# A fourth seven-product weight slab in every gate and up group, three more in the down projection, low parts subtracted by DMA

## The chip, the cores and the metric

The program runs on one core of a Trainium2 chip. The metric is device microseconds of that core for one execution. Five engines work side by side, each on its own instruction queue in a fixed order: TensorE (PE; its weight loads are shown as PEld), VectorE (DVE), ScalarE (ACT), GpSimd (POOL, which here only issues DMAs) and SyncE (SP, which issues the weight loads). A DMA moves data between memory and the on-chip buffers; an accumulating DMA adds what it reads to what lies at its destination, and only POOL issues those here.

## The reference, cut to what matters

One layer of an encoder on 256 rows of width 2048. The change touches its last third, the SwiGLU feed-forward block of inner width 5632, and the final norm behind it:

```python
def swiglu(h, w_gate_up, w_down):
    gate, up = jnp.split(h @ w_gate_up, 2, axis=-1)
    return (jax.nn.silu(gate) * up) @ w_down
...
        x = x + swiglu(rms_norm(x, norm_g[l, 2]), w_gate_up[l], w_down[l])
    return rms_norm(x, final_norm_g)
```

All arithmetic is float32. The mixers and the cross attention ahead of it are not touched.

## The kernel before

**Products.** A float32 operand is held as two parts: the high part is its rounding to the matmul's format, made by a ScalarE cast, the low part is what that rounding left, made by a VectorE subtraction. One product of two operands is three matmuls into the same PSUM bank: high by high, high by the weight's low part `wl`, low by high (`part`, L433 to L435). In the feed-forward block the activations are the stationary side (128 rows by 128) and the weights move, 512 columns at a time.

**Slabs and halves.** The weights come in 252 slabs of 16 blocks of 128x128 (1 MB), in the order of use. `Stream` loads a slab into one of three `raw` tiles and makes `wh` (ScalarE cast) and `wl` (VectorE subtraction) from it in pieces called halves. `_fill` (L167 to L171) writes out the instructions for the half that is used next and for three more; `_buffers` has three pairs of buffers in `wp` and one in the extra pool, so four halves exist at a time, and the cast of a half waits until TensorE has used up the half four before it.

**Plain slabs (N).** Two halves of 1024 columns. A slab is four activation tiles k by one group of 512 columns c; with two blocks of 128 rows each, it is 8 products, 24 matmuls.

**Paired slabs (S).** A slab is two tiles k by both column groups, again 8 block products, done in seven by a Strassen-like scheme: 21 matmuls. The sums of weight blocks that this needs are made in `_sums` (L140 to L163), the sums of activation blocks once for each pair of tiles in `combine` (tiles `z`, in the profile also `y`). A paired slab has four halves of 1024, 512, 1024 and 1024 columns, for 2, 1, 2 and 2 products. Ahead of the third half stand the additions of weight blocks on VectorE, in place in `raw`, so they wait for the casts and subtractions of the first two halves. Where the slab's number is in `SUMMED` (all paired gate and up slabs) DMAs have made part of the sums in a tile `two`: two loads on SP and one accumulating DMA on POOL (L101, L102), issued one slab ahead; two additions are left. Otherwise (the down slabs) there are four.

**Order.** `paired_rows` goes through a string of N and S. The feed-forward block has 11 groups of gate and up columns; the first goes by plain slabs, the other ten by `GROUP`, eight slabs each. In a group `mixed` (L1064 to L1071) takes the four PSUM banks of the seven-product sums out on VectorE after the last S, `gated` and `upped` (L1073 to L1084) add the other four, apply SiLU and multiply, and `up` (L1057 to L1062) turns the result on VectorE and stores it to the DRAM tensor `hidden`: twelve VectorE instructions in all. Two sets of four banks swap their roles from group to group. The down projection is two passes of 22 slabs, `PASSES`, of which the last three slabs (LATE) are left for `down_end`.

**Reloaded tiles.** `fetch` (L1087 to L1103) brings `hidden` back in the turned layout, 44 tiles `f[k]`: a load on POOL (`load_turned`), a cast on ScalarE and a subtraction on VectorE (`split`), the first 22 during the gate and up groups, the rest as the first down pass asks for them (`ready`). f[22] to f[27] lie in the tiles `z`, f[28] to f[43] in those of the block's input, `h3`, so they can be written only when the gate and up groups are done with them. In the down passes `combine` first adds the two parts of f[k] and f[k+1] on VectorE again.

**The scheduler.** A compiler pass lays each engine's instructions out in a fixed order, by the order in which the program states them and by when it expects them to be ready. `mark` and `keep_place` bind a stretch of instructions to the stated order.

**The end.** `down_end` adds the last blocks of one quarter of the columns through an identity matmul (`split`), runs 12 tiles f[k] (four from the stream, eight from the tiles `held`) by two blocks of rows, 72 matmuls, and norms each block of rows (`norm`).

## Time and profile before

| | |
|---|---|
| median of 3 runs | 1438.75 us (1436.18 to 1439.48) |
| the profiled execution | 1435.07 us, of which its span is 1433.3 us |
| TensorE, VectorE, ScalarE, POOL busy | 1423.0, 1146.2, 815.2, 234.8 us |
| mean granted TensorE clock | 0.999 |
| gate and up groups 2 to 11 | about 780 to 1193 us of the span |
| first and second down pass | about 1193 to 1309 and 1309 to 1407 us |

In the rows of the profile an engine's group of instructions has its line, its engine, its operation, `out<-in`, and in a timeline the start and length in us, the count, and in brackets how long the engine stood idle before it and what ended that. Neighbouring instructions overlap a little at their ends, so the distance from one start to the next is what one costs the engine.

### The profile page before, as it was taken

To read this page: it belongs to the slowest core of one execution; us is meant where nothing else is said; L and a number is where in the kernel's file an instruction comes from. 1 tells how busy PE (TensorE), PEld (TensorE's weight loads), DVE (VectorE), ACT (ScalarE), POOL (GpSimd) and SP (SyncE) were. 2 spreads that over 40 slices of the span, in tenths; PEclk is the share of its full clock that TensorE was granted. 3 is DMA by queue.
4 is the path that set the end of the run, shared out by engine and by line. 5 is a ranking of instruction groups with operands and counts; after the bars stand their busy time and mean duration, and the time that the engine had idled before them with its cause. 6 is when DMAs were issued, how large, how long until landed. Compare 5 with 4: busy or idle time off the path is not lost.

```text
span 1433.3 us, 18652 instructions
## 1 busy us (share of the span) xinstructions
PE 1423.0 (99%) x6589; PEld 1180.7 (82%) x6589; DVE 1146.2 (80%) x1738; ACT 815.2 (57%) x1183; POOL 234.8 (16%) x306
## 2 busy tenths in 40 slices
PE   9999999999999999999999999999999999999997
PEld 8888888888888888888888888888888888888886
DVE  6667868777877767777677888898888888989997
ACT  7556565446645555556554656555555556655655
POOL 0000100013212223531431121122011002000000
PEclk9999999999999999999999999999999999999999
DMA  9876564546667788964986999889999887655554
GB/s 352 299 285 248 205 206 162 175 169 224 202 196 236 234 267 252 274 200 166 289 239 209 286 286 277 278 275 282 294 293 288 268 260 229 219 230 179 193 218 147
DMA packets 73037, 343.79 MB, mean 240 GB/s; under 512 B 10957, under 2 KB 12654, under 8 KB 45168
## 3 DMA queue, kind: packets, MB, share of 16 engines
q1 hardware_dynamic: 54848, 288.98, 57.5%
q0 software_dynamic: 17664, 52.97, 15.8%
q8 instruction: 51, 0.84, 0.2%
q10 hardware_dynamic: 432, 0.66, 0.1%
q14 instruction: 42, 0.34, 0.1%
HBM read 322.12 MB, written 20.45 MB: 239 GB/s over the span
## 4 chain that ended last, share of the span: by engine, by line
PE 97%; DVE 1%; ACT 0%; DMA 0%; issue 0%; SPq 0%; ACTq 0%
PE pg L433 22%; PE pg L434 22%; PE pg L435 22%; PE pm L434 7%; PE pm L435 7%; PE pm L433 7%; PE pg L381 4%; PE pg L382 2%; PE pm L1344 1%; PE pm L1022 1%; PE pm L993 1%; DMA raw<-in_W 0%; PE pm L1753 0%; DVE res L283 0%; PE pm L994 0%
## 5 line engine op out<-in xcount | busy, mean ns | idle before, releaser
L136 DVE TENSOR_TENSOR wl<-raw,wh 128x1024 fp32r<-128x1024 f32 (+1 forms) x413 | 494.8, 1212 | 166.1 <-ACT wh L135 163.2
L135 ACT CAST wh<-raw 128x1024 fp32r<-128x1024 f32 (+1 forms) x413 | 424.5, 1043 | 283.9 <-PE pg L435 196.4
L433 PE MATMUL pg<-wh,act 128*128 128x512 f32 (+1 forms) x1191 | 465.6, 391 | 0.0
L434 PE MATMUL pg<-wl,act 128*128 128x512 f32 (+1 forms) x1191 | 463.9, 389 | 0.4 <-DVE wl L136 0.2
L435 PE MATMUL pg<-wh,act 128*128 128x512 f32 (+1 forms) x1191 | 463.9, 389 | 0.0
L433 PEld LDWEIGHTS pg<-wh,act 128*128 128x128 f32 x1191 | 223.8, 188 | 47.8 <-issue 1.5
L434 PEld LDWEIGHTS pg<-wl,act 128*128 128x128 f32 x1191 | 223.8, 188 | 47.2 <-DVE wl L136 1.3
L435 PEld LDWEIGHTS pg<-wh,act 128*128 128x128 f32 x1191 | 223.7, 188 | 47.2 <-DVE act L283 0.4
L159 ACT CAST wh<-raw 128x1024 fp32r<-128x1024 f32 (+1 forms) x150 | 137.0, 921 | 146.8 <-DVE raw L157 46.4
L160 DVE TENSOR_TENSOR wl<-raw,wh 128x1024 fp32r<-128x1024 f32 (+1 forms) x150 | 156.1, 1061 | 57.0 <-ACT wh L159 56.8
L434 PE MATMUL pm<-wl,act 128*128 128x512 f32 x309 | 120.5, 390 | 0.1
L433 PE MATMUL pm<-wh,act 128*128 128x512 f32 x309 | 120.2, 389 | 0.0
L435 PE MATMUL pm<-wh,act 128*128 128x512 f32 x309 | 120.2, 389 | 0.0
L381 PE MATMUL pg<-act,wh 128*128 128x512 f32 x256 | 90.5, 395 | 0.0
L382 PE MATMUL pg<-act,wl 128*128 128x256 f32 x256 | 71.8, 280 | 0.0
L434 PEld LDWEIGHTS pm<-wl,act 128*128 128x128 f32 x309 | 58.0, 188 | 13.0 <-DVE wl L136 0.6
L433 PEld LDWEIGHTS pm<-wh,act 128*128 128x128 f32 x309 | 58.0, 188 | 12.0
L435 PEld LDWEIGHTS pm<-wh,act 128*128 128x128 f32 x309 | 58.0, 188 | 12.0
L102 POOL DMA_DIRECT2D two<-in_W x30 | 26.6, 887 | 241.2 <-DMA two<-in_W 116.0
L157 DVE TENSOR_TENSOR raw<-raw 128x512 f32<-128x512 f32 x90 | 62.0, 689 | 1.3
L159 ACT CAST wh<-two 128x1024 fp32r<-128x1024 f32 x30 | 31.6, 1052 | 51.1 <-PE pg L435 21.7
L381 PEld LDWEIGHTS pg<-act,wh 128*128 128x128 f32 x256 | 48.1, 188 | 10.5
(375 smaller groups left out, 1821.9 us busy)
## 6 DMA issues: line engine op xcount, KB each, us to landing
raw<-in_W SPq DMA_DIRECT2D x216, 1024.0 KB, 5.6
raw<-in_W SPq DMA_DIRECT2D x30, 768.0 KB, 6.1
two<-in_W SPq DMA_DIRECT2D x60, 256.0 KB, 4.9
two<-in_W POOLq DMA_DIRECT2D x30, 512.0 KB, 9.3
raw<-in_W SPq DMA_DIRECT2D x11, 512.0 KB, 7.6
hidden<-g POOLq DMA_DIRECT2D x22, 256.0 KB, 3.7
tmp<-hidden POOLq DMA_DIRECT2D x44, 128.0 KB, 5.4
features<-tmp POOLq DMA_DIRECT2D x32, 128.0 KB, 5.3
```

Of the source, the lines that this page charges most:

```text
L102: nc.gpsimd.dma_start(t, W[:, 512:1536], accum_op=ALU.add)
L135: nc.scalar.copy(wh[:, a:b], r[:, a:b])
L136: nc.vector.tensor_tensor(out=wl[:, a:b], in0=r[:, a:b], in1=wh[:, a:b].bitcast(F32), op=ALU.subtract)
L157: nc.vector.tensor_tensor(out=out, in0=a, in1=b, op=ALU.add)
L159: nc.scalar.copy(wh, src)
L160: nc.vector.tensor_tensor(out=wl, in0=src, in1=wh.bitcast(F32), op=ALU.subtract)
L381: self.nc.tensor.matmul(p[:, :], wh, slot[:, :], start=start, stop=False)
L382: self.nc.tensor.matmul(p[:, 0:R], wl, slot[:, 0:R], start=False, stop=stop)
L433: self.nc.tensor.matmul(p, hi, wh, start=start, stop=False)
L434: self.nc.tensor.matmul(p, hi, wl, start=False, stop=False)
L435: self.nc.tensor.matmul(p, lo, wh, start=False, stop=stop)
L993: nc.tensor.matmul(p[:, :], q[d][:, r * P:(r + 1) * P], kt[d][:, :], start=d == 0, stop=False)
```

## The change

- **Groups.** `GROUP` goes from `NNSNSNSN` to `NSNSsNSN`: four of eight slabs in seven products. The small s is a paired slab outside `SUMMED`: loaded whole, its four additions made on VectorE. A fourth combination tile `z3` is added, made from h3[6] and h3[7]; tiles 8 to 15 instead of 6 to 15 are left to the plain slabs.
- **Down passes.** Eight and ten paired slabs instead of six and nine. The plain slabs of the first pass begin at f[16] instead of f[12].
- **Low parts by DMA.** `split_far` casts the high part on ScalarE, writes the negated operand to the low part on ScalarE, and adds the operand by an accumulating DMA on POOL. It replaces the VectorE subtraction for all 44 reloaded tiles (in no kept place) and in the combinations of the down passes. Those also take their operands from `hidden` by two loads on POOL instead of two additions on VectorE.
- **Order.** Each product of `paired_rows` is kept in its stated place. In `down_end` each block of rows is, and the identity matmuls move from ahead of the first block of rows to ahead of the second.

```diff
-GROUP = "NNSNSNSN"
+GROUP = "NSNSsNSN"
-PASSES = "NNNNSNNSNNSNNSNNSNNSNN", "NSNSNSNSNSNSNSNSNSNNNN"
+PASSES = "NNNNSNSNSNNSNSNSNNSNSN", "NSNSNSNSSNSNSNSNSSNNNN"
...
-          for i, x in enumerate(plan) if x == "S"}
-SUMMED = {i for i in PAIRED if i < DOWN}
+          for i, x in enumerate(plan) if x in "Ss"}
+SUMMED = {GATE_UP + 8 * j + i for j in range(10) for i, x in enumerate(GROUP) if x == "S"}
...
+    def split_far(self, hi, lo, src):
+
+        self.nc.scalar.copy(hi, src)
+        self.nc.scalar.mul(lo, src, -1.0)
+        self.nc.gpsimd.dma_start(lo, src, accum_op=ALU.add)
+
...
-    def combine(self, z, a, b):
+    def combine(self, z, a, b, src=None):
 
         tt, t, u, v, w = self.tt, *(self.tmp() for _ in range(4))
-        for x, y in ((t, a), (u, b)):
-            tt(x, y[:, 0:R].bitcast(F32), y[:, R:512].bitcast(F32), ALU.add)
-        yield SOON
+        if src:
+            for x, k in zip((t, u), src):
+                self.load_turned(x, self.ff, k)
+            yield 8.0
+        else:
+            for x, y in ((t, a), (u, b)):
+                tt(x, y[:, 0:R].bitcast(F32), y[:, R:512].bitcast(F32), ALU.add)
+            yield SOON
...
-        self.split2(hi[:, 0:R], lo[:, 0:R], v)
+        split = self.split_far if src else self.split2
+        split(hi[:, 0:R], lo[:, 0:R], v)
...
+            mark = self.mark()
             self.part(q[name][:, :], hi, lo, wh, wl, new, left[name] == 0)
+            self.keep_place(mark)
...
-                    mark = self.mark()
-                    self.split(f[k - ahead], m.pop(k - ahead))
-                    self.keep_place(mark)
+                    t = f[k - ahead]
+                    self.split_far(t[:, 0:R], t[:, R:512], m.pop(k - ahead))
...
-        sums = [((2 * i, 2 * i + 1), z[i]) for i in range(GROUP.count("S"))]
+        z = z + [gp.tile([P, 1024], F32R, name="z3")]
+        sums = [((2 * i, 2 * i + 1), z[i]) for i in range(4)]
...
-                yield from self.combine(x, *(f[k] for k in ks))
+                yield from self.combine(x, *(f[k] for k in ks), ks)
...
-        mark = self.mark()
-        for j, parts in split:
-            for a in parts:
-                nc.tensor.matmul(ps[1][:, j:j + R], self.identr, a, start=False, stop=False)
-        self.keep_place(mark)
...
         for r in range(2):
+            mark = self.mark()
+            for j, parts in split if r else ():
+                for a in parts:
+                    nc.tensor.matmul(ps[1][:, j:j + R], self.identr, a, start=False, stop=False)
             for k, wh, wl in held:
                 self.part_rows(ps[r], r, f[k], wh, wl, False, k == FT - 1)
+            self.keep_place(mark)
             norm(ps[r], r)
```

More of the change, by code (lines that the diff above doesn't have):

```diff
@@ L449, in combine @@
         hi, lo, x4 = self.forms(z, a)
-        self.split2(hi[:, 0:R], lo[:, 0:R], v)
+        split = self.split_far if src else self.split2
+        split(hi[:, 0:R], lo[:, 0:R], v)
         if hi.shape[1] == 512:
-            self.split2(hi[:, R:512], lo[:, R:512], w)
+            split(hi[:, R:512], lo[:, R:512], w)
         else:
-            self.split2(hi[:, R:], lo[:, R:], w[:, 0:P])
-            self.split2(*x4, w[:, P:R])
+            split(hi[:, R:], lo[:, R:], w[:, 0:P])
+            split(*x4, w[:, P:R])
     def forms(self, z, a):
@@ L490, in paired_rows @@
                 before(i)
-            if kind == "S":
+            if kind in "Ss":
                 ks, z = next(todo)
```

## The prediction

> **What bounds the kernel now.** I read the page first, then the stretches of the feed-forward block, then timelines of one paired slab and of one group's end.
>
> ```profile
> span 1433.3 us, 18652 instructions
> PE 97%; DVE 1%; ACT 0%; DMA 0%; issue 0%; SPq 0%; ACTq 0%
> 780.00:1193.00 413.00, 412.94 (x1821) 341.31 (x1820) 354.52 (x417) 233.28 (x270) 67.55 (x79) 1.00 0.90 277
> 1157.20:1198.70 41.50, 41.50 (x185) 34.37 (x184) 35.30 (x42) 23.19 (x25) 2.51 (x4) 1.00 0.70 228
> 1193.00:1309.00 116.00, 115.97 (x509) 94.80 (x508) 107.05 (x176) 68.33 (x102) 12.98 (x15) 1.00 0.63 212
> 1309.00:1407.00 98.00, 98.00 (x434) 81.12 (x434) 94.09 (x133) 56.69 (x69) 0.00 (x0) 1.00 0.57 210
> ```
>
> The chain that ended last is 97% TensorE. The rows of stretches give length, then busy us (count) of PE, PEld, DVE, ACT, POOL, the granted clock, DMA share and GB/s. TensorE has no gap in the gate and up groups (first row), and the clock is full. VectorE is busy 86% there, 92% in the first down pass, 96% in the second. So matmuls taken out shorten the time, one for one, as long as VectorE keeps ahead.
>
> ```profile
> 1396.78 0.39 PE L433 MATMUL pg<-wh,f 128*128 128x512 f32 x1
> 1401.54 0.39 PE L433 MATMUL pm<-wh,act 128*128 128x512 f32 x1
> 1151.60 0.39 PE L433 MATMUL pm<-wh,act 128*128 128x512 f32 x1
> 1193.08 0.39 PE L433 MATMUL pg<-wh,f 128*128 128x512 f32 x1
> ```
>
> The first two rows are the first matmuls of the last paired slab of the second down pass and of the plain slab behind it: 4.76 us for 21 matmuls, 0.2267 us each. The other two bound the last gate and up group: 41.48 us for 183, the same 0.2267. A product (three matmuls) is 0.68 us, a plain slab 5.44.
>
> **The gain.** Ten gate and up slabs and three down slabs lose a product each: 13 x 0.68 = 8.84 us (6.80 and 2.04). The identity matmuls only move.
>
> **VectorE on average.** One cycle of the second down pass, plain then paired, in its steady state:
>
> ```profile
> 1386.82 1.05 ACT L159 CAST wh<-raw 128x1024 fp32r<-128x1024 f32 x1 [1.17 <-PE pm L435]
> 1388.18 2.00 ACT L135 CAST wh<-raw 128x1024 fp32r<-128x1024 f32 x2 [0.31 <-PE pm L435]
> 1397.02 1.05 ACT L159 CAST wh<-raw 128x1024 fp32r<-128x1024 f32 x1 [1.17 <-PE pm L435]
> 1387.90 1.23 DVE L160 TENSOR_TENSOR wl<-raw,wh 128x1024 fp32r<-128x1024 f32 x1 [0.82 <-ACT wh L159]
> 1389.26 2.36 DVE L136 TENSOR_TENSOR wl<-raw,wh 128x1024 fp32r<-128x1024 f32 x2
> 1391.54 1.82 DVE L160 TENSOR_TENSOR wl<-raw,wh 128x1024 fp32r<-128x1024 f32 x2
> 1393.28 2.87 DVE L157 TENSOR_TENSOR raw<-raw 128x512 f32<-128x512 f32 x4
> 1396.06 1.22 DVE L160 TENSOR_TENSOR wl<-raw,wh 128x1024 fp32r<-128x1024 f32 x1
> 1398.10 1.23 DVE L160 TENSOR_TENSOR wl<-raw,wh 128x1024 fp32r<-128x1024 f32 x1 [0.82 <-ACT wh L159]
> ```
>
> From start to start, a 1024-column subtraction costs VectorE 1.14 us (1389.26 to 1391.54 is two), the 512-column one 0.60, the four additions 2.78. A paired slab with four additions is 3 x 1.14 + 0.60 + 2.78 = 6.80 us of VectorE for 4.76 us of TensorE; a plain slab 2.28 for 5.44. So s for N adds 4.52 us of VectorE to a group: the last group goes from 35.30 to 39.8 of 40.8 us, 98%, where no reloaded tile falls. Earlier groups also lose the subtraction for their reloaded tiles, 22 of them to this stage:
>
> ```profile
> L291 ACT CAST f<-tmp x14: 400/401/403, 880.2 to 1010.2; 128x256 fp32r<-128x256 f32 x14
> L283 DVE TENSOR_TENSOR f<-tmp,f x14: 414/419/422, 881.4 to 1011.6; 128x256 fp32r<-128x256 f32 x14
> L283 DVE TENSOR_TENSOR tmp<-f 128x256 f32<-128x256 f32 x6 | 2.5, 419 | 0.0
> L283 DVE TENSOR_TENSOR y<-tmp,y 128x256 fp32r<-128x256 f32 (+1 forms) x6 | 2.1, 351 | 0.0
> L283 DVE TENSOR_TENSOR f<-tmp,f 128x128 fp32r<-128x128 f32 x3 | 0.9, 288 | 0.0
> ```
>
> At 0.42 us each that is 9 us over six groups (and as much in the first down pass). In the down passes a combination loses two additions and its low parts, 2.5 + 2.1 + 0.9 = 5.5 us for three, 1.8 each, by the last three rows here. Nine old ones give 16.5 us back against three more slabs at 4.52; so the down passes end with less VectorE work, and there the trade holds on average. In the gate and up groups it holds on average too, by 1 us a group. The average isn't what decides, I think; the four buffers are.
>
> **Two paired slabs in a row (`Ss` in each group, `SS` twice in the second pass).** Call T the start of a paired slab on TensorE. The slab at 1396.78 gets its fourth low part at 1398.10, T+1.32: its cast waited for a buffer that TensorE frees as it enters the slab (1397.02, "PE"). The slab before started ten us earlier (45 matmuls, at 1386.58), and behind it the next half's subtraction began at 1389.26, T+2.68, because its cast at 1388.18 again waited for TensorE. So however idle VectorE was, it starts on the next slab at T+2.68. Where that is a paired slab with four additions: first half done at 3.82, second at 4.42, additions at 7.20, third half at 8.42. TensorE wants that third low part after 21 + 9 matmuls and one more: T+4.76+2.04+0.23 = 7.03. It is 1.39 late. If the scheduler puts two additions behind the third half, the fourth half pays: all of it on VectorE ends at T+9.56, wanted at 8.39, 1.17 late. Nothing covers this: the order of the products is kept, so TensorE can't take a later one first. I take 1.3 us (1.17 to 1.39): ten groups 13.0 us (11.7 to 13.9), two places in the second pass 2.6 (2.3 to 2.8).
>
> **The group's head.** Before, two plain slabs stood behind a group's end; now a paired one is second.
>
> ```profile
> 1151.70 1.22 DVE L136 TENSOR_TENSOR wl<-raw,wh 128x1024 fp32r<-128x1024 f32 x1
> 1152.83 0.68 DVE L283 TENSOR_TENSOR g<-g,pg 128x512 f32<-128x512 f32 x1
> 1153.43 1.28 DVE L283 TENSOR_TENSOR h<-h,pg 128x512 f32<-128x512 f32 x2
> 1154.63 1.41 DVE L287 SCALAR_TENSOR_TENSOR h<-h,rc,g 128x512 f32<-128x512 f32 x2
> 1155.95 1.30 DVE L557 STREAM_TRANSPOSE g<-h 128x512 f32<-128x512 f32 x2
> 1157.17 1.19 DVE L136 TENSOR_TENSOR wl<-raw,wh 128x1024 fp32r<-128x1024 f32 x1
> ```
>
> TensorE begins the group at 1151.60 = E (third row of the matmuls above). VectorE works without a gap through the last group's evacuation and turning until 1157.17, E+5.57. The half at 1151.70 is the third of the new group, now the paired slab's first. Behind the burst come its second half (0.60), two additions (0.70 each), third and fourth half (1.14 each): third done at E+8.7, fourth at E+9.8. TensorE wants the third at 5.44+2.04+0.23 = E+7.7 and the fourth at 9.07: some 1.0 late. Bounds: 0 if the last four instructions of the burst (1154.63 to 1157.17, 2.5 us) are put behind, 1.9 if the additions stand so that the fourth cast starts after the third subtraction. I take 1.0 for the nine groups that follow such an end: 9.0 (0 to 17).
>
> **POOL, and the start of the down projection.** Each far-made part adds one POOL issue, each combination five:
>
> ```profile
> L564 POOL DMA_DIRECT2D tmp<-hidden x44 | 38.8, 889 | 53.7 <-issue 24.4 <-DMA hidden<-g 13.3 <-DVE act L283 10.0
> two<-in_W POOLq DMA_DIRECT2D x30, 512.0 KB, 9.3
> tmp<-hidden POOLq DMA_DIRECT2D x44, 128.0 KB, 5.4
> POOL two L102 <- DMA two<-in_W: 113.1, 14, 11.7
> 1206.68 0.39 PE L433 MATMUL pg<-wh,z 128*128 128x512 f32 x1
> 1203.71 0.75 DVE L283 TENSOR_TENSOR z<-tmp,z 128x256 fp32r<-128x256 f32 x2
> PEld pg L433 <- ACT act L299: 0.6, 2, 0.3
> ```
>
> 94 more issues (44 + 10 x 5) at 0.889 are 84 us of a queue that stood idle most of the stage, no loss by themselves. ScalarE gets 44 negations, at 0.40 us if they cost what the cast of that size does, and those of the combinations, in idle time too (it is busy 233 of the 413 us). An accumulating DMA of 128 KB isn't in the trace; between the load of that size and the 512 KB accumulation it lands 5.4 to 9.3 us after its issue, where the subtraction took 0.4. That matters in one place: f[22] was subtracted at 1203.71 and wanted at 1206.68, a cover of 3 us, and with eight tiles more in pairs it is wanted 5.4 us sooner. Against that, the tile `z` it lies in comes free a slab earlier, and the work is no longer bound to its place. Small waits exist already (0.6 us in the last row). I take 1.0 us, bounds 0 and 6 (one full landing).
>
> By the Trainium skill (DMA: Bandwidth & Descriptors, "Anatomy of one DMA — SWDGE (gpsimd) path") a DMA from this queue takes 2.0 us and its bytes at 436 GB/s, an estimate of 2.3 us for 128 KB; this trace's 5.4 us for such a load is over twice that, and by the page the 1.0 would be 0 and the sum 1 us lower.
>
> **The end.** The last VectorE chain was just in time:
>
> ```profile
> PEld pm L1244 <- DVE tmp L283: 0.3, 1, 0.3
> 1410.79 1.89 DVE L127 TENSOR_TENSOR held<-raw,held 128x512 fp32r<-128x512 f32 x3
> ```
>
> The identity matmuls waited 0.3 us; moving them saves at most that. But with two paired slabs ahead VectorE reaches its end chain about as late as the second `SS` made it, and what waits next is the `held` low parts, which queue on VectorE behind that chain. I take +1.0 (−0.3 to 3).
>
> **The sum.** −8.84 + 13.0 + 2.6 + 9.0 + 1.0 + 1.0 = +17.8 us. On the profiled execution's 1435.07: 1452.8. The median of the runs, 1438.75, lies 3.7 above that execution, so the forecast is 1456.5. All lower bounds give +4.9 (1443.6), all upper ones +33.9 (1472.6).
>
> **Rivals.**
>
> 1. *Faster: VectorE keeps ahead.* If the scheduler spreads the additions and the burst so that neither place stalls, all of the gain stays: 1438.75 − 8.84 = 1429.9. For it: VectorE stays below TensorE's time on average, and the second pass already ran at 96% without a loss. Against it: there each paired slab has a plain one before it, and T+2.68 is set by buffers, which no order of VectorE changes. It decides as soon as both stalls together are under 0.4 us a group. Chance 0.14. The Trainium skill (Perfetto Trace Analysis, "Identifying the Most-Contended Engine") judges VectorE by its occupancy, and by that rule alone this rival would be the forecast; the same page says under "Optimization Strategy" that a gap that repeats can mean too few buffers, and the rows of the casts agree with that.
> 2. *About the same.* `Ss` costs its lower bound, the rest nothing but for half the group heads: within 3 us of 1438.75 only if the stalls come to 6 to 12 us in all, half of what I count. Chance 0.07.
> 3. *Slower still: POOL's order.* A far-made part waits on POOL for a load (5.4 us) and ScalarE. Where it stands ahead of a `two` accumulation, this comes up to 6 us late, and the paired slab with it. Once in each of the six groups that reload tiles, 4 us each: +24 on the forecast, 1480. For it: POOL is one queue in order, and `two` lands only 9.3 us after issue. Against it: POOL already waits up to 11.7 us for the loads of `two`, and far-made parts can fall into that. Chance 0.13.
>
> The forecast itself has 0.66. A measurement of this kernel can't tell 0.2% (2.9 us) from no change. Faster 0.15, same 0.06, slower 0.79. The forecast's own range is 1443 to 1473; to leave no more than 2 in 10 out I widen it toward the first two rivals and a little toward the third: 1433 to 1477.
>
> **What would show it.** Right: in the gate and up groups, waits of TensorE's weight loads for `wl` (L160) that sum to some 15 to 30 us, in the third and fourth half of the s slab and of each group's first paired slab; a group of 42 to 44 us; TensorE's count down by 39 matmuls; two such waits in the second pass; POOL without long waits on the path. Wrong: groups of 40.8 us with no wait (rival 1); waits for `two` or for f tiles in place of `wl` (rival 3); a first down pass longer than 118 us, or an end chain more than 3 us late.

## The result and the profile after

| | before | changed |
|---|---|---|
| median of the runs (5 each) | 1436.33 us | 1538.40 us |
| lowest and highest run | 1436.10, 1439.48 | 1535.57, 1539.58 |
| span of the profiled execution | 1433.3 us | 1537.4 us |
| mean granted TensorE clock | 0.999 | 0.983 |

The changed kernel takes 1.0702 times as long (1.0683 to 1.0720): 102 us more, where 18 were forecast. The page of the changed kernel (last row: DMA issues, KB each, median us to landing):

```profile
span 1537.4 us, 18834 instructions
...
PE 1455.7 (95%) x6550; PEld 1180.1 (77%) x6550; DVE 1180.6 (77%) x1739; ACT 857.9 (56%) x1288; POOL 318.2 (21%) x400
...
PE 70%; DVE 11%; DMA 8%; issue 5%; POOL 3%; ACT 2%; SPq 0%; ACTq 0%; POOLq 0%; DVEq 0%
...
tmp<-hidden POOLq DMA_DIRECT2D x64, 128.0 KB, 6.8
```

The waits of TensorE's weight loads in it, us in total, times and longest:

```profile
PEld pg L440 <- DVE wl L160: 34.3, 29, 6.6
PEld pm L440 <- DVE wl L160: 30.2, 29, 2.4
PEld pg L439 <- ACT wh L159: 20.4, 14, 3.4
PEld pm L439 <- ACT wh L159: 20.3, 14, 3.7
```

The matmuls went from 6589 to 6550, the 39 of the plan. The chain that ended last is TensorE's for 70% in place of 97%. TensorE waits for low parts of paired slabs, as forecast, for 64 us, but also 41 us for their high parts, which ScalarE makes, and no term of the forecast stood for that. VectorE's share of the span fell from 80% to 77%, though the waits name it. The Trainium skill (Perfetto Trace Analysis, "Identifying the Most-Contended Engine") looks for the engine with the highest occupancy, and judges TensorE's headroom by, among others, the busy share of its weight loads. Both figures are 77% here, so the rule doesn't tell TensorE and VectorE apart, and it passes over ScalarE at 56%, whose work TensorE waits for too.

Stretches of the changed kernel (length, busy us and counts of PE, PEld, DVE, ACT, POOL, granted clock, DMA share, GB/s): the eighth and the fifth of the ten groups that have paired slabs, the last, the first and the second down pass.

```profile
1125.71:1171.97 46.26, 42.64 (x181) 33.48 (x180) 39.52 (x48) 24.49 (x27) 7.74 (x9) 1.00 0.85 259
976.47:1027.77 51.30, 45.63 (x181) 35.33 (x180) 39.51 (x48) 26.96 (x35) 11.17 (x13) 0.93 0.85 237
1217.70:1275.07 57.37, 45.13 (x182) 34.40 (x180) 39.59 (x50) 35.72 (x65) 27.48 (x31) 0.91 0.86 227
1275.07:1405.81 130.74, 121.03 (x506) 96.24 (x504) 100.80 (x137) 73.06 (x119) 45.31 (x51) 0.96 0.77 226
1405.81:1510.97 105.16, 98.87 (x427) 79.57 (x426) 97.73 (x126) 59.62 (x77) 5.81 (x7) 1.00 0.56 196
```

A group has 180 matmuls, 40.81 us without a wait. A group took 46 us where nothing else falls into it, 51 where reloaded tiles do, 57 at the end. VectorE has the same 39.5 us of work in all three, so its load doesn't tell them apart; ScalarE's and POOL's columns do.

Counting the matmuls of the timeline off against the plan gives each stall its place (a stall is what a stretch has over its matmuls times 0.2267 us; in the last column but one, 17.8 us stand ahead of the first matmul of the first pass, in "groups alone" 11.7):

| stalls of TensorE, us | before | changed | groups alone | far-made reloads alone | changed, own reloads | down passes alone |
|---|---|---|---|---|---|---|
| group 1 | 0 | 5.5 | 1.0 | 2.4 | 4.1 | 0 |
| groups 2 to 6 | 0.5 | 50.5 | 17.6 | 28.3 | 25.4 | 2.1 |
| groups 7 to 9 | 0.1 | 15.3 | 8.7 | 0 | 14.8 | 0.5 |
| group 10 | 0 | 16.6 | 2.9 | 16.4 | 4.9 | 0 |
| first down pass | 1.0 | 16.5 | 17.5 | 7.2 | 53.0 | 31.1 |
| second down pass | 0 | 8.6 | 0 | 0 | 10.2 | 8.6 |
| end | 0.3 | 1.0 | 1.5 | 0.3 | 1.1 | 1.0 |
| sum | 1.9 | 113.9 | 49.2 | 54.6 | 113.5 | 43.3 |

112 us more of stalls, 8.8 less of work and 1.5 of a later start of the groups come to the 104 us between the two spans, within 1. The columns further right are experiments that follow.

### The profile page after: what moved, and what is told of

It is laid out like the page before. It is cut to its first block, busy times and chain, and to the rows that moved or that the text cites. A ratio compares the mean times of both kernels' runs of the same rounds, so it can differ in the third digit from the quotient of the medians.

```text
span 1537.4 us, 18834 instructions
## 1 busy us (share of the span) xinstructions
PE 1455.7 (95%) x6550; PEld 1180.1 (77%) x6550; DVE 1180.6 (77%) x1739; ACT 857.9 (56%) x1288; POOL 318.2 (21%) x400
## 4 chain that ended last, share of the span: by engine, by line
PE 70%; DVE 11%; DMA 8%; issue 5%; POOL 3%; ACT 2%; SPq 0%; ACTq 0%; POOLq 0%; DVEq 0%
PE pg L440 17%; PE pg L441 16%; PE pg L439 16%; DMA tmp<-hidden 5%; PE pg L387 4%; DVE wl L160 4%; PE pm L440 4%; PE pm L441 3%; PE pm L439 3%; DVE wl L136 3%; PE pg L388 2%; DVE raw L157 2%; DMA hidden<-g 1%; POOL tmp L578 1%; DMA raw<-in_W 1%
## 5 line engine op out<-in xcount | busy, mean ns | idle before, releaser
L136 DVE TENSOR_TENSOR wl<-raw,wh 128x1024 fp32r<-128x1024 f32 (+1 forms) x387 | 465.2, 1213 | 168.5 <-ACT wh L135 166.5
L135 ACT CAST wh<-raw 128x1024 fp32r<-128x1024 f32 (+1 forms) x387 | 399.7, 1042 | 273.5 <-PE pg L441 197.9
L439 PE MATMUL pg<-wh,act 128*128 128x512 f32 (+1 forms) x1166 | 457.5, 393 | 5.1 <-ACT wh L159 3.9
L441 PE MATMUL pg<-wh,act 128*128 128x512 f32 (+1 forms) x1166 | 455.3, 390 | 0.0
L159 ACT CAST wh<-raw 128x1024 fp32r<-128x1024 f32 (+1 forms) x202 | 184.7, 923 | 155.6 <-DVE raw L157 58.0
L160 DVE TENSOR_TENSOR wl<-raw,wh 128x1024 fp32r<-128x1024 f32 (+1 forms) x202 | 211.6, 1066 | 71.5 <-ACT wh L159 71.0
L439 PEld LDWEIGHTS pg<-wh,act 128*128 128x128 f32 x1166 | 219.7, 188 | 54.9 <-ACT wh L159 6.5
L441 PEld LDWEIGHTS pg<-wh,act 128*128 128x128 f32 x1166 | 219.5, 188 | 45.7 <-DVE act L283 0.2
L440 PE MATMUL pm<-wl,act 128*128 128x512 f32 x284 | 113.3, 399 | 8.5 <-DVE wl L160 8.5
L439 PE MATMUL pm<-wh,act 128*128 128x512 f32 x284 | 112.9, 397 | 5.7 <-ACT wh L159 5.6
L441 PE MATMUL pm<-wh,act 128*128 128x512 f32 x284 | 111.4, 392 | 0.0
L157 DVE TENSOR_TENSOR raw<-raw 128x512 f32<-128x512 f32 x142 | 98.0, 690 | 3.1
L578 POOL DMA_DIRECT2D tmp<-hidden x64 | 61.5, 1053 | 101.1 <-ACT tmp L1172 50.7
L439 PEld LDWEIGHTS pm<-wh,act 128*128 128x128 f32 x284 | 54.3, 191 | 20.1 <-ACT wh L159 8.7
L441 PEld LDWEIGHTS pm<-wh,act 128*128 128x128 f32 x284 | 54.0, 190 | 10.8
L160 DVE TENSOR_TENSOR wl<-two,wh 128x1024 fp32r<-128x1024 f32 x30 | 36.7, 1225 | 30.1 <-ACT wh L159 30.1
```

Of the source, the lines that this page charges most:

```text
L135: nc.scalar.copy(wh[:, a:b], r[:, a:b])
L136: nc.vector.tensor_tensor(out=wl[:, a:b], in0=r[:, a:b], in1=wh[:, a:b].bitcast(F32), op=ALU.subtract)
L157: nc.vector.tensor_tensor(out=out, in0=a, in1=b, op=ALU.add)
L159: nc.scalar.copy(wh, src)
L160: nc.vector.tensor_tensor(out=wl, in0=src, in1=wh.bitcast(F32), op=ALU.subtract)
L439: self.nc.tensor.matmul(p, hi, wh, start=start, stop=False)
```

## The experiments

Medians, each with its ratio to the kernel before (which ran beside it, 1435.9 to 1437.0 us):

| kernel | median us | ratio (95%) |
|---|---|---|
| e1_groups: new groups alone | 1474.07 | 1.0261 (1.0245 to 1.0276) |
| e5_head: a pair at a group's head, three pairs | 1450.27 | 1.0098 (1.0078 to 1.0119) |
| e6_next_four: two pairs side by side, three pairs | 1447.82 | 1.0075 (1.0058 to 1.0091) |
| e16_five_next: e6 with a fifth buffer | 1446.40 | 1.0066 (1.0048 to 1.0084) |
| e17_five_head: e5 with a fifth buffer | 1456.19 | 1.0132 (1.0114 to 1.0151) |
| e18_next_later: e6, the two pairs one slab later | 1452.31 | 1.0112 (1.0095 to 1.0129) |
| e19_five_later: e18 with a fifth buffer | 1439.88 | 1.0022 (1.0013 to 1.0031) |
| e10_kept_order: kept order of products alone | 1438.65 | 1.0021 (1.0006 to 1.0035) |
| e9_free_order: changed, without the kept order | 1527.12 | 1.0622 (1.0590 to 1.0654) |
| e2_far_fetch: far-made reloads alone | 1491.24 | 1.0378 (1.0363 to 1.0394) |
| e3_own_fetch: changed, VectorE's own reloads | 1538.12 | 1.0707 (1.0683 to 1.0731) |
| e8_kept_fetch: changed, far-made reloads in kept place | 1568.65 | 1.0916 (1.0898 to 1.0935) |
| e20_fetch_on_time: e1, reloads stepped in each group | 1468.01 | 1.0216 (1.0196 to 1.0236) |
| e4_down: changed down passes alone | 1474.47 | 1.0263 (1.0240 to 1.0286) |
| e13_early_combine: e4, combinations two slabs sooner | 1468.87 | 1.0225 (1.0200 to 1.0250) |
| e15_passes: new plan of the passes alone | 1447.16 | 1.0074 (1.0055 to 1.0093) |
| e14_own_parts: e4, VectorE's low parts | 1458.60 | 1.0161 (1.0142 to 1.0180) |
| e21_own_free: e14 without the kept order | 1454.81 | 1.0124 (1.0107 to 1.0141) |

### The two places in the groups

```diff
-GROUP = "NNSNSNSN"
+GROUP = "NSNSsNSN"
```

> The kernel before with the new plan of the gate and up groups alone (NSNSsNSN); SwiGLU tiles split and combined as before. Theory T (place: four half buffers fix when VectorE can begin on the next slab): the head of a group and the Ss pair each stall, some 2.2 and 2.5 us as the changed kernel's groups without reloads show, so groups of about 45.8 us against 41.5, and a little more in the groups with reloads, where VectorE also has their subtractions: +43 us, about 1480. Rival R1 (VectorE's average): only groups with reloads pass 100% of VectorE, at most 9 us of subtraction over budget: groups without reloads 40.8 us, total 1430 to 1440. Prediction's own sizes: 22 us of stalls less 6.8, about 1451.

```diff
-GROUP = "NNSNSNSN"
+GROUP = "NSNNSNSN"
```

> The kernel before with its first paired slab of each gate and up group moved from third to second place (NSNNSNSN): the same work on every engine. Theory T (place): nine group heads stall as in the changed kernel, 2.2 us each, +20 us, about 1456. Prediction's size: 1.0 us each, +9. Rival R1 (average load): 0.

```diff
-GROUP = "NNSNSNSN"
+GROUP = "NNSsNNSN"
```

> The kernel before with its second paired slab moved next to its first and made one with four additions (NNSsNNSN): the same work for TensorE, two additions more for VectorE per group (1.4 us of 41.5). Theory T (place): ten stalls at the s slab of 2.5 us, +25 us, about 1461. Prediction's size: 1.3 us each, +13. Rival R1 (average load): VectorE goes from 85% to 88% in the groups, so 0.

With three pairs and one bad place each, the nine heads cost 1.1 to 2.0 us each (mean 1.5), the ten s slabs 1.1 to 2.1 us (mean 1.4): 13.8 and 11.3 us by the medians. So the two places exist, and the load on average (R1) is out. The prediction's 1.3 for the s slab was near, its 1.0 for the head a third too low and inside its bounds. Together, with the fourth pair, a group stalls 2.9 us (groups 7 to 10 of e1_groups: 1.8 at the head, 0.9 at the s slab), which is about the sum of the two alone; the changed kernel stalls 4.9 at the same two places. Theory T, which took the changed kernel's sizes for each place, was too high in all three.

### Buffers or backlog

The prediction held that four buffers decide, whatever VectorE did before. The edit gives groups 1 to 9 a fifth pair of buffers in a pool of its own, and lets the halves run one further ahead:

```diff
-        pool = self.extra if self.extra and len(self.halves) % 4 == 3 else self.wp
+        pool = self.extra if self.extra and self.pos % 5 == 3 else self.more if self.pos % 5 == 4 and self.more else self.wp
...
-        ahead = self.at + 1 + min(3 if self.extra else 2, self.n // 16)
+        ahead = self.at + 1 + min(4 if self.more else 3 if self.extra else 2, self.n // 16)
```

> The kernel with two paired slabs side by side (NNSsNNSN, measured 1447.8) with a fifth buffer for a half of weights in groups 1 to 9 (the last group has four again; the arrival tiles have two buffers in place of four). Theory T of the prediction (VectorE can't begin the next slab before T+2.68, since its cast waits for a buffer): the stall of 1.2 us at the s slab goes in nine groups and stays in the last: -10 us, 1437 to 1439. Rival V (VectorE's order of work at that place decides, not the buffer): 1448.

> The kernel with a paired slab second in each group (NSNNSNSN, measured 1450.3) with a fifth buffer for a half of weights in groups 1 to 9. Theory T: VectorE stands a half further ahead when the last group's burst begins, 1.14 us against a lateness of 0.3 to 1.1 us: the stalls of eight heads go, the last stays (its buffer is the fourth again): -11 us, 1438 to 1441. Rival V: 1450.

Both missed: 1.4 us less and 5.9 us more. A stretch of e16_five_next, from the eighth group's burst to behind its s slab (columns as above):

```profile
1079.00:1099.50 20.50, 19.80 (x87) 15.77 (x86) 19.82 (x26) 11.36 (x13) 5.13 (x6) 1.00 0.84 240
```

VectorE worked 19.8 of 20.5 us; it had no idle time that a buffer could give it. In e17_five_head ScalarE, a half further ahead, stood 3.4 us for the load of `raw` just ahead of the ninth group. So the pair was moved away from the burst, with four and with five buffers:

```diff
-GROUP = "NNSsNNSN"
+GROUP = "NNNSsNSN"
```

> The kernel before with two paired slabs side by side one place later in each group (NNNSsNSN in place of NNSsNNSN, measured 1447.8); the same work. Theory B (backlog: VectorE works without a gap from the burst at a group's end until the s slab, and one plain slab more, 2.3 us of VectorE for 5.4 us of TensorE, lets it catch up by 3.2 us against a lateness of 1.2): the ten stalls go, 1436 to 1438. Prediction's theory (buffers: T+2.68 whatever VectorE did before): the stalls stay, 1446 to 1450.

> The kernel of e18_next_later (NNNSsNSN) with a fifth buffer for a half of weights in groups 1 to 9. Theory B: as e18_next_later within 3 us, 1435 to 1440. Prediction's theory (buffers): the stall that stays with four buffers falls by most of its 1.2 us in nine groups, 10 us less than e18_next_later.

Here the buffers decide: the stalls stay with four (0.9 to 2.2 us a group) and fall to 0.2 to 0.5 with five, 1.4 in the last group, which had four again. The S slab of the sixth group begins on TensorE at T = 1010.57 in e18_next_later and 1003.12 in e19_five_later. ScalarE and VectorE of the first, then of the second:

```profile
1012.17 1.57 ACT L159 CAST wh<-raw 128x1024 fp32r<-128x1024 f32 x2 [0.31 <-PE pm L435]
...
1011.89 3.19 DVE L160 TENSOR_TENSOR wl<-raw,wh 128x1024 fp32r<-128x1024 f32 x3 [1.21 <-ACT wh L159]
...
1015.33 2.86 DVE L157 TENSOR_TENSOR raw<-raw 128x512 f32<-128x512 f32 x4
1018.11 1.22 DVE L160 TENSOR_TENSOR wl<-raw,wh 128x1024 fp32r<-128x1024 f32 x1
1019.25 1.22 DVE L136 TENSOR_TENSOR wl<-raw,wh 128x1024 fp32r<-128x1024 f32 x1
1020.38 1.22 DVE L160 TENSOR_TENSOR wl<-raw,wh 128x1024 fp32r<-128x1024 f32 x1
```

```profile
1004.44 1.23 DVE L164 TENSOR_TENSOR wl<-raw,wh 128x1024 fp32r<-128x1024 f32 x1 [1.49 <-ACT wh L163]
...
1006.52 2.86 DVE L161 TENSOR_TENSOR raw<-raw 128x512 f32<-128x512 f32 x4
```

With four buffers the fourth low part of S begins at T+1.32, the prediction's figure, the additions at T+4.76, and the third half of s is done some 1.14 us behind 1018.11, at T+8.7 (forecast 8.42). What the forecast lacks is the row at 1019.25: a half of the next plain slab stands between the third and the fourth half of s, so that by these rows both low parts are late, not one of them. With five buffers the additions begin at T+3.40, and 0.4 of this group's 1.2 us of stall are left. By the Trainium skill (Perfetto Trace Analysis, "Optimization Strategy") a gap that repeats can mean too few buffers; this pair of runs agrees, and the pair at NNSs shows where it doesn't hold.

### The kept order of the products

```diff
+            mark = self.mark()
             self.part(q[name][:, :], hi, lo, wh, wl, new, left[name] == 0)
+            self.keep_place(mark)
```

These lines in the kernel before are e10_kept_order; the changed kernel without them is e9_free_order.

> The kernel before with one part of the change: the kept order of the products in put. Nothing else differs. Theory T2: the order costs only where a half is late, and the kernel before has 1.9 us of such waits in all: 0 to +4 us, 1436 to 1440. Rival R4 (the order costs by itself, at every paired slab, some 1 us each): 39 paired slabs, +20 us or more.

> The changed kernel without the kept order of the products (the two lines around part in put taken out). Theory T2 (the kept order adds to every late half: TensorE may not take a product with a ready high part ahead of one whose low part is late): each Ss stall falls from 2.3 to 2.9 us to the 0.9 of the run with the new groups alone, each head from 2.2 to 1.7, the two SS of the second pass from 2.3 to about 1: some -24 us, about 1514. Rival R3 (kept order costs nothing, the difference between the two kernels' stalls comes from the far-made parts on ScalarE): 1538. The stalls in groups with reloads (far-made parts) stay in both.

Alone the order costs 0.2%, all of it in the first down pass. In the changed kernel taking it out gives 11 us (its runs lie between 1520.7 and 1528.9, so this is good to some 4 us): half of what T2 expected. The best pair for it is e1_groups and e3_own_fetch, whose groups 4 to 9 hold the same work and no reloads: 2.9 to 3.3 us of stalls without the order, 4.9 with it. TensorE at the s slab of the eighth group, in e1_groups and in the changed kernel (there `part` is L439 to L441):

```profile
1109.95 0.73 PE L433 MATMUL pg<-wh,z 128*128 128x512 f32 x2
...
1110.89 0.73 PE L433 MATMUL pm<-wh,act 128*128 128x512 f32 x2 [0.22 <-ACT wh L135]
1111.47 0.41 PE L434 MATMUL pg<-wl,z 128*128 128x512 f32 x1
```

```profile
1151.25 0.50 PE L439 MATMUL pg<-wh,z 128*128 128x512 f32 x1 [0.66 <-ACT wh L159]
1152.68 0.50 PE L440 MATMUL pg<-wl,z 128*128 128x512 f32 x1 [0.93 <-DVE wl L160]
...
1154.95 0.50 PE L440 MATMUL pm<-wl,act 128*128 128x512 f32 x1 [0.61 <-DVE wl L160]
```

Left free, the scheduler has set four matmuls that need only high parts ahead of the first that needs the late low part. Kept in order, TensorE waits with one matmul done, and again at the next half.

### Far-made low parts of reloaded tiles

```diff
-                    mark = self.mark()
-                    self.split(f[k - ahead], m.pop(k - ahead))
-                    self.keep_place(mark)
+                    t = f[k - ahead]
+                    self.split_far(t[:, 0:R], t[:, R:512], m.pop(k - ahead))
```

> The kernel before with one part of the change: the low parts of the reloaded SwiGLU tiles are far-made (cast and negation on ScalarE, accumulating DMA on POOL), in no kept place. Theory T (casts that wait for their load stand in ScalarE's in-order queue ahead of weight casts): stalls of TensorE in the groups with reloads and in the first down pass, +10 to +40 us, with waits of the casts of weights behind casts of f tiles. Rival R1 (VectorE's load decides): VectorE has 18 us less to do and TensorE had no stalls, so 0, 1436. Rival R2 (POOL's order: two comes late): about +24 us, with TensorE or POOL waiting for two instead of for weight halves.

This part alone makes the kernel 55 us slower, above T's 40, though it takes work off VectorE: the largest single cost. VectorE's load (R1) is out. The fifth group of the changed kernel, ScalarE, VectorE and TensorE:

```profile
990.12 0.41 ACT L304 CAST f<-tmp 128x256 fp32r<-128x256 f32 x1 [2.04 <-DMA tmp<-hidden]
...
996.18 0.41 ACT L304 CAST f<-tmp 128x256 fp32r<-128x256 f32 x1 [3.17 <-DMA tmp<-hidden]
...
998.26 1.03 ACT L159 CAST wh<-two 128x1024 fp32r<-128x1024 f32 x1
...
999.32 1.23 DVE L160 TENSOR_TENSOR wl<-two,wh 128x1024 fp32r<-128x1024 f32 x1 [4.57 <-ACT wh L159]
...
999.34 0.79 PE L439 MATMUL pm<-wh,z 128*128 128x512 f32 x1 [2.74 <-ACT wh L159]
```

ScalarE is idle here, but not free: its queue holds the cast of a tile whose load is under way, and behind it the cast of the weights. Once the last of these loads has landed, the cast of the tile, its negation and the weight's cast follow without a gap; so it was the loads that were late, not `two` (against R2, and against the mechanism of the prediction's rival 3): the `two` of this slab was issued at 971.20 and by the trace had landed at 982.05, 16 us ahead of its cast. The chain that ended last runs through one such load in each of groups 1 to 6, 8.2 to 8.9 us from issue to landing.

What the kept place did shows in the 22 casts of reloaded tiles in these groups. In the kernel before each starts 2.8 to 42 us behind the landing of its load, and ScalarE is never idle ahead of one. Without the place, the scheduler sets each right behind its load: within 3.0 us of the landing in e2_far_fetch, within 0.8 in the changed kernel. ScalarE's idle time ahead of these casts (us, times), in the changed kernel, then in e2_far_fetch:

```profile
DMA tmp<-hidden: 40.1, 21
...
DMA tmp<-hidden: 27.1, 8
```

The last group shows the same with more links, ScalarE, POOL and TensorE:

```profile
1256.93 0.41 ACT L304 CAST act<-tmp 128x256 fp32r<-128x256 f32 x1 [7.03 <-DMA tmp<-hidden]
...
1254.89 0.93 POOL L578 DMA_DIRECT2D tmp<-hidden  x1 [3.69 <-DMA z<-tmp]
...
1258.47 0.80 PE L439 MATMUL pg<-wh,z 128*128 128x512 f32 x1 [2.94 <-ACT wh L159]
1265.34 0.80 PE L440 MATMUL pg<-wl,z 128*128 128x512 f32 x1 [6.08 <-DVE wl L160]
```

The load waits on POOL for a `tmp` tile, which an accumulating DMA still reads.

Two kernels were to mend this: e3_own_fetch takes the edit back in the changed kernel, e8_kept_fetch sets `mark` and `keep_place` around its new lines.

> The changed kernel with the reloaded tiles split as before (VectorE's subtraction, kept place); everything else changed. Theory T: the 4 to 6 us that the far-made parts cost in each of five groups go (-25 us) and the last group's 11 us; but VectorE, at 98% of its time in the groups, gets 22 subtractions back, and in the run with the new groups alone the reloads were put off to the end of the last group and TensorE waited 12 us for the first of them: so -20 to -36 us, 1502 to 1518, with one wait of over 8 us at the start of the first down pass. Rival R1 (VectorE's average decides): the subtractions come back on the fullest engine, 1538 or more.

> The changed kernel with the kept place, which the change dropped, put back around the far-made split of a reloaded tile. Theory T (the cast of a tile whose load is still under way stands in ScalarE's in-order queue ahead of the casts of weights, because nothing holds it at its planned place): the 4 to 6 us a group that groups 2 to 6 lose beside the others fall by most, some -20 us, about 1518; the waits in the last group and the first pass stay. Rival R2 (POOL's order, two late) and rival R6 (the planned place is itself too early for the load): no change, 1538.

Both took the extra stalls out of groups 2 to 6 (25.4 and 27.0 us are left of 50.5, nearly all at the two places), but they took the tiles out as well: from the second group to the ninth neither kernel has a cast of a reloaded tile. So they don't show what far-made parts in a kept place would cost in the middle of the groups. And neither gained: 0 and +30 us. Put back in place, the tiles come late at the other end. With the new groups alone it is the same, POOL and TensorE of e1_groups:

```profile
1221.95 1.53 POOL L559 DMA_DIRECT2D hidden<-g  x2 [35.00 <-DVE g L557]
1223.45 10.58 POOL L564 DMA_DIRECT2D tmp<-hidden  x12
...
1228.21 0.80 PE L433 MATMUL pg<-wh,f 128*128 128x512 f32 x1 [11.57 <-ACT f L291]
```

Before, four reloads are issued in each of seven groups and three in an eighth; in e1_groups and e3_own_fetch four in each of the first three, and then none until these twelve, behind the last group's store. The code steps its background work only while VectorE's planned backlog is small, and with four pairs it seldom is. Stepping the reloads by hand, at each slab from the third on:

```diff
+        def on_time(i):
+            for e in [e for e in self.bg.q if e[0] is early and i > 1]:
+                self.bg.step(e)
```

> The kernel with the new groups alone (measured 1474.1), its reloads of SwiGLU tiles stepped at each slab from the third on of every group, where in the run before four each were issued in the first three groups and the rest only behind the last. Theory D (the list of background work holds a step back while VectorE is full, so the reloads come late): the 11.7 us wait at the start of the first pass and the 2.3 us of slow clock behind it go, and the subtractions that now lie in more groups cost up to 1.5 us each: -7 to -14 us, 1460 to 1467. Rival (the wait is POOL's or the load's own, issued on time or not): 1474.

The 22 casts are back in the groups, in a kept place, and none of them waits. The wait of 11.7 us and what followed it are gone (15 us of the first pass), 8 us come back in the groups, and 6 us are gained, one less than the least that was expected. Neither kind of reload was free in these groups: VectorE's own cost 8 us here, the far-made ones 31.5 in the changed kernel.

### The changed down passes

e4_down is the changed kernel with the old `GROUP` and the old `fetch`.

> The changed kernel with the old gate and up groups (three pairs, NNSNSNSN) and the old split of reloaded tiles: of the change, the 18 pairs of the down passes, the combinations from reloaded tiles with accumulating DMAs, the moved identity products and the kept order are left. Prediction's sizes: -2.0 + 2.6 + 1.0 + 1.0, so 1439. Theory T: the first pass keeps the stalls that its paired slabs 4, 6, 8 and 11 show in the changed kernel (16 us) and the second its three (8.5 us): 1436 - 2 + 25, about 1459. Rival R5 (these stalls are inherited from the late last group): 1436 to 1442.

38.5 us, and 31 of them in the first pass: more than there were in the changed kernel, so they aren't inherited (R5), and T was 15 us too low. TensorE at the first two paired slabs, and POOL between them:

```profile
1228.95 0.80 PE L441 MATMUL pg<-wh,act 128*128 128x512 f32 x1 [7.68 <-DMA act<-tmp]
...
1251.41 0.79 PE L441 MATMUL pg<-wh,act 128*128 128x512 f32 x1 [7.00 <-DMA act<-tmp]
```

```profile
1221.81 1.32 POOL L306 DMA_DIRECT2D act<-tmp  x1
...
1228.84 1.85 POOL L578 DMA_DIRECT2D tmp<-hidden  x2 [5.71 <-DMA y<-tmp]
```

The second product of a paired slab takes a low part that an accumulating DMA is still making (14.7 us in these two waits). The first was issued at 1221.8, half a microsecond after its wait began, and took the 7 us; the loads of the next combinations stand behind such DMAs for `tmp` tiles.

In the changed kernel the first pass loses its time another way. None of its waits there ends with an accumulating DMA; they end with weight halves, and ahead of the first of these stands the cast of a far-made reloaded tile, as in the groups. ScalarE and TensorE at the pass's first paired slab, which stalls 8.5 of the 16.5 us:

```profile
1298.18 0.40 ACT L304 CAST act<-tmp 128x256 fp32r<-128x256 f32 x1 [3.70 <-DMA tmp<-hidden]
...
1299.71 0.60 ACT L159 CAST wh<-raw 128x512 fp32r<-128x512 f32 x1
...
1300.36 0.50 PE L439 MATMUL pg<-wh,act 128*128 128x512 f32 x1 [2.02 <-ACT wh L159]
```

So e4_down shows what the changed passes cost by themselves, and not how the changed kernel's 16.5 us come about; how much of these the reloads make wasn't taken apart.

In e4_down the combinations were then begun two slabs sooner:

```diff
-                while plan[j] == "S" and len(made) <= plan[:j].count("S"):
+                while len(made) < plan[:j + 3].count("S"):
```

> The kernel with the changed down passes alone (measured 1474.5), its combinations begun two slabs sooner: each must be issued before the second slab ahead of its paired slab, not before that slab. Theory L (latency: load 5.5 us, VectorE, ScalarE, then an accumulating DMA of 4 to 7 us, one behind the other, and TensorE waits at the product that takes the last low part): 11 us of cover hides most of the 7 to 8 us waits at the paired slabs 4 and 6, -15 to -25 us, about 1455. Rival B (the tmp buffers and POOL's queue are the bound: what is begun sooner waits sooner): within 5 us of 1474.

Those two waits go, others come in their place (5.9 us at the second paired slab for a half of weights, 3.4 at the third plain slab for a reloaded tile), and 5.6 us are gained in all: nearer to rival B. The parts one by one:

> The kernel before with the new plan of the two down passes alone (18 pairs in place of 15); the combinations are VectorE's, from the tiles that are on the chip, as before. Theory L (reloads and accumulating DMAs cost the 38 us of the changed down passes): VectorE has 13.6 us more for three slabs and some 6 more for combinations over 211 us, and the two SS places stall about 1 us each: 1436 to 1443. Theory B (VectorE is full: 107 of 116 us in the first pass, two slabs and their combinations more make it 120 of 114): the first pass loses 6 to 12 us, 1443 to 1450. Theory P (the plan itself costs the 38): 1465 to 1475.

> The kernel with the changed down passes alone (measured 1474.5), the low parts of its combinations made by VectorE in place of the negation and the accumulating DMA; the reloads stay. Theory A (the accumulating DMA's 4 to 7 us at the end of each combination make it late; TensorE waits 16 us for it in the first pass): -12 to -20 us, 1455 to 1462. Theory R (the reload and the queue of loads for tmp buffers make it late): within 5 us of 1474. VectorE's own load would cost up to 1.8 us for each of 18 combinations in either.

> The kernel with the changed down passes alone and VectorE's low parts (measured 1458.6), without the kept order of the products: against the plan of pairs alone (1447.2) it differs by the reloads and the moved identity products. Theory R (the reloads cost most of the 11 us, the kept order little): 1454 to 1459. Rival K (the kept order costs most: with it TensorE waits in place for a late combination): 1447 to 1451.

The edits are the line `PASSES` alone; `split = self.split2` in `combine`; and that without the two lines around `part`. The plan costs 10.5 us: 2.0 are gained, and the second pass stalls 8.7 us in three places, 5 at its first paired slab (waits of 2.2 and 1.4, and slow matmuls behind them), 1.1 and 1.8 at the two SS; the first pass stalls 3 us more than before. The first pass ends on SN now instead of NN: its evacuation on VectorE goes on until 5.5 us into the second pass in e15_passes, against 2.2 us in the kernel before, and so falls against that pass's first paired slab. The reloads and the changed end (the moved identity products, the kept order of each block of rows) add 7.7 us (e21 to e15), the kept order 3.8 (e14 to e21), the accumulating DMAs 15.9 (e4 to e14). The sum is e4's 38.

## Why the prediction was wrong

The direction was right, the size off by 82 us, and 1538 lies far above the range. Its steps:

| step | forecast | in the changed kernel |
|---|---|---|
| the gain, 39 matmuls | −8.8 | −8.8 |
| two paired slabs in a row, ten groups | +13.0 | +22.9 |
| the group's head, nine groups | +9.0 | +20.6 |
| far-made reloads in groups 1 to 6 | 0 | +31.5 |
| POOL and the start of the down projection (last group, first pass) | +1.0 | +11.6, +15.5 |
| SS twice in the second pass | +2.6 | +4.9 |
| the second pass's first paired slab | 0 | +3.7 |
| the end | +1.0 | +0.7 |
| later start of the groups | 0 | +1.5 |

The right column takes the stalls place by place, slow matmuls behind a wait included; with 1.3 us in small places it adds to the 104 us between the spans, within 1.

- *The gain* was right to the matmul.
- *Two paired slabs in a row, and the head.* Right in mechanism and, alone, near in size (1.4 and 1.5 us against 1.3 and 1.0). The two terms are mis-sized by 21 us together; the places alone make some 5 of these, and one thing most of the rest. The step "Nothing covers this: the order of the products is kept, so TensorE can't take a later one first" was used only to say that lateness counts; that the order turns one late half into two waits wasn't priced (2.0 us a group, e1_groups to e3_own_fetch; 11 us for the whole kernel by e9_free_order). That both places lie in one group, where VectorE works 39.5 of 40.8 us, moves the stall from the s slab to the head (1.4 and 1.5 us alone, 0.9 and 1.8 in e1_groups) and adds nothing to the sum.
- *"The four buffers are"* what decides held at NNNSsNSN alone. Right behind a group's end VectorE's backlog decides, and a fifth buffer there gains 1.4 us or loses 5.9.
- *"94 more issues … no loss by themselves", and ScalarE's added work "in idle time too".* This step failed first and cost most. It counted issues and negations, 0.9 and 0.4 us each, and never asked where a cast stands that waits for a load, although the change took its kept place away. 31.5 us in the groups and part of the last one's 11.6 and the first pass's 15.5. Taking the step back alone gains nothing, though (e3_own_fetch): the tiles then come late at the groups' end, and stepped on time VectorE's own cost 8 us (e20_fetch_on_time).
- *"That matters in one place: f[22]"*, with bounds of 0 and one landing. Accumulating DMAs stand at the end of every combination, and there are ten of these (not the 18 of e14_own_parts' expectation), with a reload (6.8 us) at the head of each. That is a chain of latencies for each, and the forecast gave it one price once: by e4_down these passes cost 38.5 us alone, 15.9 of them for the accumulating DMAs. In the changed kernel's first pass TensorE waits for weight halves instead, first for one behind a reload in ScalarE's queue. "On average" VectorE does gain in these passes, as the step said; what the gain is traded for was left out.
- *Rival 3* had the place (reloads in six groups), nearly the size (+24, against the 25 us that groups 2 to 6 lose beyond those of e3_own_fetch, which have no such cast), and the wrong queue.
- *Rivals 1 and 2* fell with the first run: the order that the scheduler chose spared neither place.
- *"A first down pass longer than 118 us"* was named as what would show it wrong: it took 130.7.

None of the runs beats the kernel before. The nearest with paired slabs side by side, e19_five_later, saves no product and stands at 1.0022; a fourth pair with a fifth buffer wasn't tried. How much of the last group's 11.6 us is the reloads' own and how much the combinations', wasn't taken apart.

## What to carry to other kernels

An operation moved from a busy engine to a DMA costs that engine nothing and the consumer a latency: price it at each consumer (here load, cast, negation, accumulating DMA, 6.8 us and 5.1 to 9.1 for the two DMAs alone, by their medians), and look at what stands behind the waiting instruction in each in-order queue and which ring of tiles it holds. An ordering constraint that costs 0.2% while nothing is late costs several times that once something is, so constraints and stalls are to be priced together. And where a wait has two possible causes, buffers and backlog, move the place rather than only add a buffer: the first test alone would have thrown out a mechanism that was right one slab further on.

## What the hardware showed that was not expected

Behind the long waits TensorE runs at half speed for a while. The first matmuls behind the wait of 7.7 us in e4_down, with a granted clock of 0.51 from 1229.0 to 1231.9:

```profile
1229.54 0.63 PE L439 MATMUL pg<-wh,act 128*128 128x512 f32 x1
1229.97 0.63 PE L440 MATMUL pg<-wl,act 128*128 128x512 f32 x1
1230.40 0.63 PE L441 MATMUL pg<-wh,act 128*128 128x512 f32 x1
...
1232.21 0.39 PE L440 MATMUL pm<-wl,y 128*128 128x512 f32 x1
1232.44 0.39 PE L441 MATMUL pm<-wh,y 128*128 128x512 f32 x1
```

They start 0.43 us apart in place of 0.227. In the changed kernel 68 matmuls stand so, 0.2 us each, 13 us in all; the granted clock of its last group is 0.91. The waits ahead of them were as short as 2.0 us with a second of 1.0 one matmul later, and the same pair of waits left the clock alone in one group of e2_far_fetch and brought up to 13 slow matmuls in another. The Trainium skill (TensorE: Matmul & The Clock Gate, "What's actually happening") has the clock halved after an idle window of about 3.4 us that runs on its own, whatever the kernel does; half speed and the chance in it agree with these rows. The length doesn't: here two shorter waits, 3.0 us in all with a matmul between them, were enough, and in e2_far_fetch 1.6 and 1.0.

An accumulating DMA takes about as long to land as a plain load of its size. DMA issues of the changed kernel (KB each, median us from issue to landing):

```profile
tmp<-hidden POOLq DMA_DIRECT2D x64, 128.0 KB, 6.8
...
act<-tmp POOLq DMA_DIRECT2D x24, 128.0 KB, 6.5
...
f<-tmp POOLq DMA_DIRECT2D x14, 128.0 KB, 6.5
...
y<-tmp POOLq DMA_DIRECT2D x10, 128.0 KB, 5.1
...
z<-tmp POOLq DMA_DIRECT2D x6, 128.0 KB, 9.1
```

Each replaced a subtraction of 0.42 us. The plain load's own median, 5.4 us before, doesn't follow from them: it is 7.5 us in e1_groups, which has none of these DMAs, and 5.5 in e4_down, which has those of the combinations.
